# Two transformer layers on one core: where the streamed activations lie relative to the weights, modulo 128 bytes

## The chip, the core and the metric

The kernel runs on one core of a Trainium2 chip. The metric is the device time of one launch in microseconds. The kernel before took 2894.02 us, the median of three runs (2893.97, 2894.02 and 2896.38 us). A profile of one further execution stands beside them; where lines of the kernel are named (L213), they are those of the kernel before.

## What is computed

The input x has 256 tokens of 2048 numbers. Two layers follow each other. The first puts 16 learned tokens ahead, mixes with an RWKV-7 recurrence beside a causal attention, and ends with a gated feed-forward part. The second mixes with a long convolution (Hyena) beside a latent attention, and ends with a feed-forward part whose gate passes through a 3-tap convolution. Cut to the products that matter here:

```python
proj = rms(h) @ w_in                                   # 2048 x 10704
merged = g_a * (y_a @ w_branch_a) + g_b * (y_b @ w_branch_b)
h = h + merged @ w_o                                   # 2048 x 2048
gate, up = split(rms(h) @ w_gate_up)                   # 2048 x 11264
h = h + (silu(gate) * up) @ w_down                     # 5632 x 2048
proj = rms(h) @ w_in_2                                 # second layer
h = h + rms(concat(rms(y_hyena), rms(y_attn)) @ w_out_2)
g, u = split(rms(h) @ w_up_2)                          # 2048 x 11264
h = h + rms((gelu(conv3(g)) * u) @ w_down_2)           # 5632 x 2048
```

All is float32. Nearly all of the time goes into these dense products.

## The kernel before

**Split products.** TensorE multiplies numbers of reduced precision (fp32r), so each float32 operand is split into a high part (a rounded copy) and a low part (the rest). A product is three matmuls into the same PSUM bank (`mm3`, L213 to L215): weights high times activations high, weights low times activations high, weights high times activations low. The weights are the stationary operand, a 128x128 tile that LDWEIGHTS loads; the activations stream past as the moving operand, 256 columns (one per token) in most stages, 272 or 258 in the first product.

**The weight stream.** A weight matrix is cut into pieces of 8 tiles of 128x128 (512 KB). `stream` walks over the pieces and `weights` brings each: SP issues its DMA into `wr`, ScalarE casts it into `wh` (L195), VectorE subtracts into `wl` (L196). Each of the three has a pool of three buffers (`wraw`, `whi`, `wlo`) that all stages share. One piece feeds 8 x 3 = 24 matmuls. `weights` runs at high priority, so a scheduler puts the casts and subtractions well ahead of the rest of a stage; the order on each engine is fixed when the program is built.

**The stages**, in order: the first product (w_in, with the RWKV and attention work among it), `phase_merge` (w_ab, then w_o in `run`), `phase_glu` (w_gu, 176 pieces), w_down in `run` (176 pieces), `phase_mix` (w_in2 with the work of Hyena and of the latent attention), `phase_out` (w_out2), `phase_conv_glu` (w_up2, 176 pieces; its first four blocks run as one group while `bring` makes the normed activations) and `phase_last` (w_down2, 176 pieces). In `phase_last` the roles are turned: the hidden activations `hh` are stationary, 128 tokens at a time, and the weights move, 512 columns at a time (L925 to L927, 1056 matmuls).

**Where the operands lie.** A tile has the same byte address in every partition, and an allocator places tiles of a pool one behind the other. The helper `act` makes an activation tile 32 numbers (128 bytes) longer than needed and starts `off` numbers into it. `wr`, `wh` and `wl` start at 32 modulo 128 bytes in all their buffers, and each tile and each block of 256 columns is a multiple of 128 bytes long, so one number describes a stage: the start of the moving operand less that of the stationary one, modulo 128. This is called the **offset** below. In the built program before the change it is:

| stage | moving operand | matmuls | offset |
|---|---|---|---|
| w_in | xh, xl (272, 258 or 256 columns) | 5520 | changes by 64 from one k to the next |
| w_ab | yah, yal, ybh, ybl | 768 | 0 |
| w_o | mh, ml | 768 | 48 |
| w_gu | x2h, x2l | 4224 | 32 |
| w_down | hh, hl | 2112 | 64 |
| w_in2 | x3h, x3l | 1488 | 16 |
| w_q2, w_k2, w_v2 | hyh, hyl, huh, hul (w_v2: weights) | 216 | 0 |
| w_out2 | yhh, yhl, yah2, yal2 | 768 | 64 |
| w_up2 | x4h, x4l | 4224 | 96 |
| w_down2 | weights, 512 columns | 1056 | 96 |

The names yah and yah2 read alike in a profile (yah): before 1000 us it is the tile of w_ab, after 2000 us that of w_out2.

Of the kernel before, what the change touches and what calls it, by code (L numbers as in the profile page):

```python
# [12 lines left out]
F32R = mybir.dt.float32r  # L13
# [5 lines left out]
P = 128  # L19
D = 2048  # L20
KT = D // P
S = 256
# [6 lines left out]
HT = HID // P  # L29
C0 = math.exp(-0.5)  # L30
BIG = 1e30
PIECE = 8
# [118 lines left out]
class Builder:  # L151
# [21 lines left out]
    def act(self, pool, tag, off):  # L173

        return self.tl(pool, [P, KT * S + 32], tag, F32R)[:, off : off + KT * S].rearrange("p (k s) -> p k s", k=KT)

# [40 lines left out]
    def stream(self, name):  # L217

        w = self.a[name]
        for i in range(w.shape[0]):  # L220
            wh, wl = self.weights(w[i], PIECE)
            for k in range(PIECE):
                yield wh[:, k], wl[:, k]
# [78 lines left out]
    def run(self):  # L302
# [13 lines left out]
        al = slice(0, S)  # L316
        spill = nc.dram_tensor("spill_h", (P, KT, S), F32, kind="Internal").ap()
        spill2 = nc.dram_tensor("spill_h2", (P, KT, S), F32, kind="Internal").ap()
        with ExitStack() as right:
# [4 lines left out]
            with ExitStack() as pa:  # L324
                ph = ExitStack()
                php = self.pool(ph, "ph", side="right")
                self.h = self.tl(php, [P, KT, S], "h")
                pm = ExitStack()
                pmp = self.pool(pm, "pm", side="right")
                mh = self.act(pmp, "mh", 28)  # L330
                ml = self.act(pmp, "ml", 28)
                pf = ExitStack()
                filters = self.filters(pf)
                self.phase_merge(pa, mh, ml, filters)
            with ExitStack() as pb:
                xp = self.pool(pb, "x2")
                xh = self.act(xp, "x2h", 8)
                xl = self.act(xp, "x2l", 8)
# [15 lines left out]
            with ExitStack() as pc:  # L354
                xp = self.pool(pc, "x3")
                xh = self.act(xp, "x3h", 4)
                xl = self.act(xp, "x3l", 4)
                st = self.stream("w_down")
                for i in range(KT):
                    ps = self.bank()  # L360
                    self.dense(ps, st, HT, hh, hl, al)
                    self.residual(i, ps, "pre", xh, xl)
                    if i % 4 == 3:
                        nc.scalar.dma_start(out=spill[:, i - 3 : i + 1], in_=self.h[:, i - 3 : i + 1])
# [9 lines left out]
            with ExitStack() as pe:  # L374
                xp = self.pool(pe, "x4")
                xh = self.act(xp, "x4h", 24)
                xl = self.act(xp, "x4l", 24)
                php = self.pool(pe, "ph2")
                self.h = self.tl(php, [P, KT, S], "h")
                nc.scalar.dma_start(out=self.h, in_=spill)  # L380
                with ExitStack() as pf:
                    bring = self.phase_out(pf, ys, rs, xh, xl)
                    py.close()
                    pd = ExitStack()
                    hp = self.pool(pd, "hp2", side="right")
                    hh = self.tl(hp, [P, HT, S], "hh2", F32R)
                    hl = self.tl(hp, [P, HT, S], "hl2", F32R)
                    self.tl(hp, [P, 8], "shift")
                    self.phase_conv_glu(xh, xl, hh, hl, bring, spill2)
                self.dump("h3", self.h)  # L390
# [111 lines left out]
    def phase_merge(self, pa, mh, ml, filters):  # L502
        nc, a = self.nc, self.a
        al = slice(0, S)
        w = self.pool(pa, "pmgy")
        w2 = self.pool(pa, "pmg", 2)
        ys = []
# [31 lines left out]
    def phase_glu(self, xh, xl, hh, hl):  # L539
# [3 lines left out]
        with ExitStack() as c:  # L543
            w2 = self.pool(c, "pglu", 2)
            st = self.stream("w_gu")
# [319 lines left out]
    def phase_conv_glu(self, xh, xl, hh, hl, bring, spill):  # L865
# [3 lines left out]
        with ExitStack() as c:  # L869
            w2 = self.pool(c, "pcg", 2)  # L870
            st = self.stream("w_up2")
# [3 lines left out]
            for i in range(0, KT, 4):  # L875
                nc.scalar.dma_start(out=spill[:, i : i + 4], in_=self.h[:, i : i + 4])

# [521 lines left out]
```

## Time and profile before

| | |
|---|---|
| runs | 2893.97, 2894.02, 2896.38 us |
| profiled execution | 2894.61 us |
| its span, first to last instruction | 2892.8 us |
| mean granted TensorE clock | 0.995 |
| weight pieces: cast on ScalarE, subtraction on VectorE | 1045 ns and 1223 ns (mean of 872) |
| DMA of a piece of w_gu, issue to landing | 3.5 us (median) |

The profile's page gives busy time by engine, the chain of work that ended last and the costliest groups of instructions. For this change the most telling view is another: the busy time and the number of matmuls in a stretch of time. Where TensorE is busy all through, the length of the stretch over the number of matmuls that start in it is their spacing. The duration of one matmul in the other views is longer, since matmuls are pipelined and overlap.

### The profile page before, as it was taken

Reading aid. Unit: us, or ns where it says so; the run is one execution under the profiler, and the core shown is the slowest. Engines: PE = TensorE matmul, PEld = TensorE weight load, DVE = VectorE, ACT = ScalarE, POOL = GpSimd, SP = SyncE. Lnnn points to the kernel's source line nnn. Section 1 sums busy time; section 2 is a strip of 40 time slices with the busy share of each in tenths; the row PEclk is TensorE's granted clock in tenths of the full one; section 3 lists DMA queues with packets and bytes.
Section 4 is the critical chain, followed back from the end, with each engine's and each line's share of the span. In section 5 each row is a group of like instructions: output and inputs, shape, how many; then the busy total and the mean of one; then the engine's idle time right before and its main releaser. Section 6 shows DMA issues by size and latency. Waiting matters only on the chain.

```text
span 2892.8 us, 56251 instructions
## 1 busy us (share of the span) xinstructions
PE 2855.3 (99%) x23286; PEld 2688.2 (93%) x23286; DVE 1854.1 (64%) x2948; ACT 1340.9 (46%) x1998; POOL 184.8 (6%) x339
## 2 busy tenths in 40 slices
PE   8999999999999999999999999999989999999998
PEld 7988888888999999999999999999989999998886
DVE  8856666776566655555555556687786666665444
ACT  6544555555444444444444445444454444444433
POOL 4000000000000200000000000010220000000000
PEclk9999999999999999999999999999999999999999
DMA  6433333334676555555555666444655555556554
GB/s 209 135 113 112 99 116 106 114 105 134 194 241 200 185 183 188 184 186 186 185 187 199 202 200 216 160 144 146 198 177 187 185 187 183 189 184 222 187 188 160
DMA packets 147617, 497.23 MB, mean 172 GB/s; under 512 B 16224, under 2 KB 30816, under 8 KB 146784
## 3 DMA queue, kind: packets, MB, share of 16 engines
q1 hardware_dynamic: 128448, 458.42, 48.7%
q10 hardware_dynamic: 18272, 33.12, 3.3%
q8 instruction: 182, 2.98, 0.4%
q0 software_dynamic: 640, 2.10, 0.3%
q14 instruction: 75, 0.61, 0.1%
HBM read 478.37 MB, written 15.20 MB: 171 GB/s over the span
## 4 chain that ended last, share of the span: by engine, by line
PE 95%; DVE 2%; DMA 1%; ACT 1%; issue 0%; SPq 0%; POOL 0%; ACTq 0%; DVEq 0%; POOLq 0%
PE psd L215 12%; PE psd L213 12%; PE psd L214 12%; PE psb L213 5%; PE psb L215 5%; PE psa L215 5%; PE psc L213 5%; PE psa L213 5%; PE psc L214 5%; PE psc L215 5%; PE psb L214 5%; PE psa L214 4%; PE psd L926 1%; PE psd L925 1%; PE psa L926 1%; PE psa L925 1%
## 5 line engine op out<-in xcount | busy, mean ns | idle before, releaser
L196 DVE TENSOR_TENSOR wl<-wr,wh 128x1024 fp32r<-128x1024 f32 (+1 forms) x872 | 1065.9, 1223 | 668.5 <-ACT wh L195 667.4
L195 ACT CAST wh<-wr 128x1024 fp32r<-128x1024 f32 (+1 forms) x872 | 910.5, 1045 | 1241.5 <-PE psd L215 353.4
L214 PE MATMUL psd<-xh,wl 128*128 128x256 f32 (+2 forms) x1280 | 371.5, 290 | 0.2 <-DVE wl L196 0.2
L215 PE MATMUL psd<-xl,wh 128*128 128x256 f32 (+2 forms) x1280 | 371.4, 290 | 0.0
L213 PE MATMUL psd<-xh,wh 128*128 128x256 f32 (+2 forms) x1280 | 369.9, 289 | 0.6 <-DVE p L1000 0.6
L213 PEld LDWEIGHTS psd<-xh,wh 128*128 128x128 f32 x1280 | 241.2, 188 | 8.6 <-issue 4.1
L215 PEld LDWEIGHTS psd<-xl,wh 128*128 128x128 f32 x1280 | 241.1, 188 | 7.8 <-issue 3.2
L214 PEld LDWEIGHTS psd<-xh,wl 128*128 128x128 f32 x1280 | 240.9, 188 | 5.7 <-DVE wl L196 0.4
L213 PE MATMUL psd<-x3h,wh 128*128 128x256 f32 x496 | 141.3, 285 | 0.0
L215 PE MATMUL psd<-x3l,wh 128*128 128x256 f32 x496 | 140.5, 283 | 0.0
L214 PE MATMUL psd<-x3h,wl 128*128 128x256 f32 x496 | 139.8, 282 | 0.0
L256 POOL TENSOR_TENSOR acc<-acc,ssq 128x256 f32<-128x256 f32 x56 | 72.2, 1290 | 859.9 <-ACT ssq L258 859.8
L213 PE MATMUL psa<-x4h,wh 128*128 128x256 f32 x352 | 99.8, 284 | 3.8 <-ACT x4h L246 3.8
L214 PE MATMUL psa<-x4h,wl 128*128 128x256 f32 x352 | 99.7, 283 | 2.7 <-DVE wl L196 2.7
L215 PE MATMUL psa<-x4l,wh 128*128 128x256 f32 x352 | 99.3, 282 | 1.4 <-DVE x4l L247 1.0
L213 PE MATMUL psb<-x4h,wh 128*128 128x256 f32 x352 | 99.4, 282 | 0.0
L213 PE MATMUL psc<-x4h,wh 128*128 128x256 f32 x352 | 99.4, 282 | 0.0
L213 PE MATMUL psd<-x4h,wh 128*128 128x256 f32 x352 | 99.4, 282 | 0.0
L215 PE MATMUL psa<-x2l,wh 128*128 128x256 f32 x352 | 99.2, 282 | 0.0
L213 PE MATMUL psa<-x2h,wh 128*128 128x256 f32 x352 | 99.2, 282 | 0.0
L214 PE MATMUL psd<-x4h,wl 128*128 128x256 f32 x352 | 99.1, 282 | 0.0
L214 PE MATMUL psb<-x4h,wl 128*128 128x256 f32 x352 | 99.1, 282 | 0.0
(664 smaller groups left out, 8476.2 us busy)
## 6 DMA issues: line engine op xcount, KB each, us to landing
wr<-w_in_dram SPq DMA_DIRECT2D x230, 512.0 KB, 3.4
wr<-w_gu_dram SPq DMA_DIRECT2D x176, 512.0 KB, 3.5
wr<-w_down_dram SPq DMA_DIRECT2D x176, 512.0 KB, 3.5
wr<-w_up_dram SPq DMA_DIRECT2D x176, 512.0 KB, 3.5
wr<-w_ab_dram SPq DMA_DIRECT2D x32, 512.0 KB, 4.3
wr<-w_o_dram SPq DMA_DIRECT2D x32, 512.0 KB, 3.4
wr<-w_out_dram SPq DMA_DIRECT2D x32, 512.0 KB, 4.3
spill_g<-gate ACTq DMA_DIRECT2D x32, 128.0 KB, 2.7
```

Of the source, the lines that this page charges most:

```text
L195: self.nc.scalar.copy(hi, src)
L196: self.nc.vector.tensor_tensor(out=lo, in0=src, in1=hi.bitcast(F32), op=ALU.subtract)
L213: nc.tensor.matmul(out, lhsT=wh, rhs=xh, start=start, stop=False)
L214: nc.tensor.matmul(out, lhsT=wl, rhs=xh, start=False, stop=False)
L215: nc.tensor.matmul(out, lhsT=wh, rhs=xl, start=False, stop=stop)
L256: nc.gpsimd.tensor_tensor(out=acc, in0=acc, in1=self.pending[id(acc)], op=ALU.add)
L925: nc.tensor.matmul(ps[b], lhsT=hh[:, k, bs], rhs=wh[:, q], start=k == 0, stop=False)
L926: nc.tensor.matmul(ps[b], lhsT=hh[:, k, bs], rhs=wl[:, q], start=False, stop=False)
```

## The change

`act` is gone, and with it the numbers 28, 8, 4 and 24. Each activation pool of a streamed stage gets either nothing or a small tile `shift` of 64 bytes first, so that the operands lie at an offset of 64. The pool of hh2 loses its 32-byte `shift`. In the built program the offset is 64 in every row of the table above but w_in, whose rows stay as they were.

Second, `stream` takes a list of pieces that go "away": their high and low parts get a buffer of their own, outside the three, which lies at 96 modulo 128 as the activations do, so that these pieces are multiplied at an **offset of 0**. They are pieces 2, 6, 40 and 100 of w_gu, piece 2 of w_down and pieces 10, 14, 48 and 100 of w_up2: 9 of 528, 216 matmuls. Their raw data still pass through `wraw`.

Third, in `phase_conv_glu` the pool of `phase_out` (`pmo`, with `mix`) is closed after the group and before the pools `pcgw` and `pcg` are opened, so the away buffer and the tiles of the convolution (`conv_p`, `cg`, `cu`) lie where `mix` was.

```diff
-    def act(self, pool, tag, off):
-
-        return self.tl(pool, [P, KT * S + 32], tag, F32R)[:, off : off + KT * S].rearrange("p (k s) -> p k s", k=KT)
-
...
-    def stream(self, name):
+    def shift(self, pool):
+
+        self.tl(pool, [P, 16], "shift")
+
+    def stream(self, name, away=(), pool=None):
+
 
         w = self.a[name]
         for i in range(w.shape[0]):
-            wh, wl = self.weights(w[i], PIECE)
+            if i in away:
+                wh, wl = self.weights(w[i], PIECE, (self.wraw, pool[0], pool[0]), tag="aw")
+            else:
+                wh, wl = self.weights(w[i], PIECE)
             for k in range(PIECE):
                 yield wh[:, k], wl[:, k]
...
-                mh = self.act(pmp, "mh", 28)
-                ml = self.act(pmp, "ml", 28)
+                mh = self.tl(pmp, [P, KT, S], "mh", F32R)
+                ml = self.tl(pmp, [P, KT, S], "ml", F32R)
...
-                xh = self.act(xp, "x2h", 8)
-                xl = self.act(xp, "x2l", 8)
+                self.shift(xp)
+                xh = self.tl(xp, [P, KT, S], "x2h", F32R)
+                xl = self.tl(xp, [P, KT, S], "x2l", F32R)
...
-                xh = self.act(xp, "x3h", 4)
-                xl = self.act(xp, "x3l", 4)
-                st = self.stream("w_down")
...
+                self.shift(xp)
+                xh = self.tl(xp, [P, KT, S], "x3h", F32R)
+                xl = self.tl(xp, [P, KT, S], "x3l", F32R)
+                with ExitStack() as c:
+                    st = self.stream("w_down", (2,), [self.pool(c, "pdn")])
...
-                xh = self.act(xp, "x4h", 24)
-                xl = self.act(xp, "x4l", 24)
+                self.shift(xp)
+                xh = self.tl(xp, [P, KT, S], "x4h", F32R)
+                xl = self.tl(xp, [P, KT, S], "x4l", F32R)
...
-                    self.tl(hp, [P, 8], "shift")
-                    self.phase_conv_glu(xh, xl, hh, hl, bring, spill2)
...
+                self.phase_conv_glu(xh, xl, hh, hl, bring, spill2, pf)
...
         w = self.pool(pa, "pmgy")
+        self.shift(w)
...
+            st = self.stream("w_gu", (2, 6, 40, 100), [self.pool(c, "pgl")])
             w2 = self.pool(c, "pglu", 2)
-            st = self.stream("w_gu")
...
-            w2 = self.pool(c, "pcg", 2)
-            st = self.stream("w_up2")
+            pool = []
+            st = self.stream("w_up2", (10, 14, 48, 100), pool)
             first = [self.bank() for _ in range(4)]
             self.group(first, st, KT, xh, xl, [al] * 4, bring)
             self.rstd(R, self.total(self.acc), S, 1.0 / D, 1e-6)
             for i in range(0, KT, 4):
                 nc.scalar.dma_start(out=spill[:, i : i + 4], in_=self.h[:, i : i + 4])
+            pf.close()
+            pool.append(self.pool(c, "pcgw"))
+            w2 = self.pool(c, "pcg", 2)
```

The order of instructions on TensorE is the same in both programs; only the names of the away tiles differ. On TensorE at piece 2 of w_gu, the end of piece 1 and the start of piece 2 now read (xh and xl of w_gu are x2h and x2l; the numbers are those of buffers):

```order
L211 MATMUL psa_12702<-x2l_11580,wh_12734 128x256
L209 MATMUL psa_12702<-x2h_11579,wh_12734 128x256
L210 MATMUL psa_12702<-x2h_11579,wl_12735 128x256
L211 MATMUL psa_12702<-x2l_11580,wh_12734 128x256
L209 MATMUL psb_12766<-x2h_11579,awh_12768 128x256
L210 MATMUL psb_12766<-x2h_11579,awl_12769 128x256
L211 MATMUL psb_12766<-x2l_11580,awh_12768 128x256
```

Nothing moved there: before, the same rows hold wh_12763 and wl_12764 in place of awh and awl.

On ScalarE at the end of w_o, the casts of w_gu's pieces 0, 1 and 2 (before: wh_12699, wh_12729 and wh_12763) stand among the last residuals:

```order
L195 CAST wh_12699<-wr_12698 128x1024
L258 ACTIVATE ssq_12604<-h_10059 128x256
L246 ACTIVATE x2h_11577<-h_10059,cols_61 128x256
L195 CAST wh_12729<-wr_12728 128x1024
L195 CAST wh_12763<-wr_12762 128x1024
L258 ACTIVATE ssq_12671<-h_10059 128x256
```

With the change they are wh_12704, wh_12734 and awh_12768:

```order
L191 CAST wh_12704<-wr_12703 128x1024
L262 ACTIVATE ssq_12606<-h_10059 128x256
L250 ACTIVATE x2h_11579<-h_10059,cols_61 128x256
L191 CAST awh_12768<-wr_12767 128x1024
L191 CAST wh_12734<-wr_12733 128x1024
L191 CAST wh_12798<-wr_12797 128x1024
```

The cast of the away piece, piece 2, now stands ahead of that of piece 1, which TensorE needs first; the subtractions on VectorE follow the same order.

On GpSimd, where `bring` adds up squares (acc, ssq) and `conv_p` gets its two zero columns, the memsets of the first two conv_p tiles stood ahead of the last additions:

```order
L256 TENSOR_TENSOR acc_86<-acc_86,ssq_25531 128x256
L563 MEMSET conv_p_25994 128x1
L564 MEMSET conv_p_25994 128x1
L563 MEMSET conv_p_26008 128x1
L564 MEMSET conv_p_26008 128x1
L256 TENSOR_TENSOR acc_86<-acc_86,ssq_25657 128x256
```

Now they stand behind all of them:

```order
L260 TENSOR_TENSOR acc_86<-acc_86,ssq_25929 128x256
L260 TENSOR_TENSOR acc_86<-acc_86,ssq_25948 128x256
L571 MEMSET conv_p_26009 128x1
L572 MEMSET conv_p_26009 128x1
L571 MEMSET conv_p_26023 128x1
L572 MEMSET conv_p_26023 128x1
```

Four memsets moved past fourteen additions, since their tiles now lie where `mix` was.

More of the change, by code (lines that the diff above doesn't have):

```diff
@@ L355, in run @@
                 xp = self.pool(pc, "x3")
-                xh = self.act(xp, "x3h", 4)
-                xl = self.act(xp, "x3l", 4)
-                st = self.stream("w_down")
[L359 to L364, printed above, removed]
+                self.shift(xp)
[3 more added lines that the diff above has]
+                    st = self.stream("w_down", (2,), [self.pool(c, "pdn")])
+                    for i in range(KT):
+                        ps = self.bank()
+                        self.dense(ps, st, HT, hh, hl, al)
+                        self.residual(i, ps, "pre", xh, xl)
+                        if i % 4 == 3:
+                            nc.scalar.dma_start(out=spill[:, i - 3 : i + 1], in_=self.h[:, i - 3 : i + 1])
                 pd.close()
@@ L380, in run @@
                 nc.scalar.dma_start(out=self.h, in_=spill)
[L381 to L387, printed above, removed]
-                    self.tl(hp, [P, 8], "shift")
-                    self.phase_conv_glu(xh, xl, hh, hl, bring, spill2)
+                pf = ExitStack()
+                bring = self.phase_out(pf, ys, rs, xh, xl)
+                py.close()
+                pd = ExitStack()
+                hp = self.pool(pd, "hp2", side="right")
+                hh = self.tl(hp, [P, HT, S], "hh2", F32R)
+                hl = self.tl(hp, [P, HT, S], "hl2", F32R)
+                self.phase_conv_glu(xh, xl, hh, hl, bring, spill2, pf)
                 self.dump("h3", self.h)
@@ L863, in phase_out, with phase_conv_glu @@
         return bring
-    def phase_conv_glu(self, xh, xl, hh, hl, bring, spill):
+    def phase_conv_glu(self, xh, xl, hh, hl, bring, spill, pf):
         nc, a = self.nc, self.a
```

## The prediction

> **What bounds the kernel now.** I read the page first: its line of busy times, the clock by slices, the chain of work that ended last.
>
> ```profile
> PE 2855.3 (99%) x23286; PEld 2688.2 (93%) x23286; DVE 1854.1 (64%) x2948; ACT 1340.9 (46%) x1998; POOL 184.8 (6%) x339
> PEclk9999999999999999999999999999999999999999
> PE 95%; DVE 2%; DMA 1%; ACT 1%; issue 0%; SPq 0%; POOL 0%; ACTq 0%; DVEq 0%; POOLq 0%
> ```
>
> TensorE is busy for 2855 of 2892.8 us at a clock that is nearly always granted in full, and it makes up 95% of the chain. But a busy TensorE need not run at its peak, so the question is how far apart matmuls start. The view of busy time by stretches answers it. Its columns are the stretch, its length, busy us and (x instructions) of TensorE, of its weight load, VectorE, ScalarE and GpSimd, then clock and DMA.
>
> ```profile
> 802.00:830.00 28.00, 28.00 (x236) 28.00 (x235) 17.96 (x25) 11.47 (x15) 0.00 (x0) 1.00 0.82 260
> 956.00:1016.00 60.00, 60.00 (x522) 60.00 (x521) 40.08 (x44) 30.86 (x44) 15.41 (x11) 1.00 0.61 197
> 1020.00:1516.00 496.00, 496.00 (x4186) 495.95 (x4185) 284.59 (x352) 213.31 (x265) 0.00 (x0) 1.00 0.58 185
> 1521.00:1757.00 236.00, 236.00 (x2085) 236.00 (x2084) 124.74 (x118) 102.36 (x117) 19.54 (x14) 1.00 0.61 200
> 1771.50:1781.50 10.00, 10.00 (x87) 10.00 (x86) 7.88 (x10) 6.14 (x10) 3.05 (x2) 1.00 0.87 290
> 2156.00:2630.00 474.00, 474.00 (x4002) 474.00 (x4001) 325.71 (x473) 203.61 (x255) 5.56 (x84) 1.00 0.57 185
> 2660.00:2880.00 220.00, 220.00 (x944) 176.98 (x944) 98.28 (x83) 86.19 (x91) 0.00 (x0) 1.00 0.54 179
> ```
>
> The count also holds the two or so matmuls that were still running when a stretch began (one lasts about 280 ns at a spacing near 118), so I take 2.4 off, and 1.7 for 512 columns. Spacings by stage: w_ab, offset 0: 28/233.6 = 119.9 ns. w_o, 48: 60/519.6 = 115.5. w_gu, 32: 496/4183.6 = 118.6. w_down, 64: 236/2082.6 = **113.3**. w_in2, 16: 10/84.6 = 118.2. w_up2, 96: 474/3999.6 = 118.5. w_down2, 96 at 512 columns: 220/942.3 = 233.5. In w_gu, w_down and w_up2 the clock is 1.00, TensorE never idle, the matmuls 256 wide and the weights from the same buffers. What differs in the table of offsets is only where the moving operand lies. The one at 64 is the fastest. The durations of single matmuls say the same:
>
> ```profile
> L213 PE MATMUL psc<-x4h,wh 128*128 128x256 f32 x352 | 99.4, 282 | 0.0
> L213 PE MATMUL psd<-x2h,wh 128*128 128x256 f32 x352 | 99.0, 281 | 0.0
> L213 PE MATMUL psc<-hh,wh 128*128 128x256 f32 x176 | 48.6, 276 | 0.0
> ```
>
> So TensorE's spacing is the bound, and offset 64 can be had for 113.3 ns. But not always. Two stretches of w_out2, whose offset is 64 as well, grouped by line and shape (count | busy us, mean ns of one):
>
> ```profile
> L214 PE MATMUL psb<-yah,wl 128*128 128x256 f32 x7 | 2.0, 281 | 0.0
> L215 PE MATMUL psb<-yal,wh 128*128 128x256 f32 x7 | 2.0, 281 | 0.0
> ...
> L214 PE MATMUL psc<-yhh,wl 128*128 128x256 f32 x13 | 3.6, 276 | 0.0
> L215 PE MATMUL psb<-yal,wh 128*128 128x256 f32 x8 | 2.2, 276 | 0.0
> ```
>
> The first two rows are from 2024.2 to 2026.7 us, the others from 2036 to 2046 us. The same tile yal takes 281 ns in the one and 276 in the other. The timeline of the first stretch gives its spacing:
>
> ```profile
> 2024.36 0.28 PE L215 MATMUL psb<-yal,wh 128*128 128x256 f32 x1
> ...
> 2026.83 0.28 PE L215 MATMUL psb<-yal,wh 128*128 128x256 f32 x1
> ```
>
> Between these starts lie 21 matmuls: 2.47/21 = **117.6 ns**, held for the whole group. So offset 64 has two modes, a fast one (113.3) and a slow one (117.6), and the slow one is worth hardly more than offsets 32 or 96 (118.5). Whatever came before a run picks the mode. This decides the case.
>
> **The change part by part**, in the fast mode:
>
> *w_gu*: 176 pieces x 24 = 4224 matmuls. 4128 go from 118.6 to 113.3: 5.3 x 4128 = 21.9 us. The 96 of the four level pieces go from 118.6 to 119.9 (the row of w_ab): +0.1. Gain 21.8. In the slow mode it would be 1.0 x 4128 - 0.1 = 4.0.
>
> *w_up2*: the first 192 matmuls are the group that waits for `bring`:
>
> ```profile
> 2121.00:2154.00 33.00, 28.71 (x201) 27.08 (x202) 31.74 (x52) 19.64 (x41) 13.20 (x14) 0.90 0.46 160
> ```
>
> There VectorE is busy for 31.74 of 33 us and TensorE waits for it, so nothing is gained. Of the other 4032, 3936 gain 118.5 - 113.3 = 5.2: 20.5, less 0.1 for the level pieces: 20.4.
>
> *w_down2*, 512 columns: no run at offset 64 is in the trace. At offset 0 there is one, w_v2, whose timeline shows
>
> ```profile
> 1827.27 0.39 PE L649 MATMUL psa<-wl,huh 128*128 128x512 f32 x1
> ...
> 1829.99 0.39 PE L649 MATMUL psa<-wl,huh 128*128 128x512 f32 x1
> ```
>
> 12 matmuls in 2.72 us: 226.7 ns. The 256 further columns thus cost 226.7 - 119.9 = 106.8 over the 256-wide matmul at the same offset; added to 113.3 that estimates 220.1 at offset 64. Gain: (233.5 - 220.1) x 1056 = 14.2 us. Bounds: nothing, if it stays at 233.5; and twice 106.8 = 213.6, columns alone, 21.0. I take 220.1 because it uses the row of the same width. The Trainium skill, page "TensorE: Matmul & The Clock Gate", section "Back-to-back issue gap", puts a warm matmul at columns/2.4 + 2.5 ns, that is 215.8 for 512; by that the gain would be 18.7. No run here shows that spacing at 512 columns.
>
> *w_ab*: 768 matmuls, 119.9. The first half runs unbroken, 384 x 6.6 = 2.5; the second half is broken by the filters' own matmuls, which stay as they are, so I count the slow mode there: 384 x 2.3 = 0.9. Sum 3.4; bounds 1.8 and 5.1.
> *w_o*: only the last 540 run unbroken: 2.2 x 540 = 1.2; bounds -1.1 (slow) and 1.7.
> *w_in2, w_q2, w_k2*: 1680 matmuls at 118 to 120 between attention and Hyena work. Half of them at 113.3: 840 x 4.9 = 4.1, of which I keep 3.3 since TensorE also waits for others there; bounds 0 and 8.2.
> *w_down* is at 64 already; its level piece costs 24 x 6.6 = 0.2. *w_out2*: nothing. Both lose if their mode turns slow: 4.3 x 2088 = 9.0 and 4.3 x 768 = 3.3.
>
> *Order.* The away piece's cast stands ahead of piece 1's on ScalarE. Piece 1 comes 1.05 us (cast) later, and its subtraction 1.22 us; TensorE works 24 x 113 = 2.7 us on piece 0 meanwhile. I count 1 us for one stall (bounds 0 and 2.3). The memsets of conv_p moved behind `bring`'s additions: the last addition ends at 2148.75 and VectorE first writes conv_p at 2156.51, so four memsets of one column each have 7.8 us, under the chain of the normalisation: nothing.
>
> ```profile
> 2147.62 1.13 POOL L256 TENSOR_TENSOR acc<-acc,ssq 128x256 f32<-128x256 f32 x1 [1.62 <-ACT ssq L258]
> 2156.51 0.42 DVE L565 TENSOR_TENSOR conv_p<-psa,R 128x256 f32<-128x256 f32 x1
> L195 ACT CAST wh<-wr 128x1024 fp32r<-128x1024 f32 (+1 forms) x872 | 910.5, 1045 | 1241.5 <-PE psd L215 353.4
> L196 DVE TENSOR_TENSOR wl<-wr,wh 128x1024 fp32r<-128x1024 f32 (+1 forms) x872 | 1065.9, 1223 | 668.5 <-ACT wh L195 667.4
> ```
>
> *Supply.* At 113.3 a piece lasts 2.72 us, which w_down is fed at already, without idle time on TensorE. VectorE does more beside it in w_up2: 325.71 of 474 us, which becomes 72% of 453. w_down2 would use a piece in 12 x 220 = 2.64 us. That is enough.
>
> Sum: 21.8 + 20.4 + 14.2 + 3.4 + 1.2 + 3.3 - 0.2 - 1.0 = **63.1 us**. The profiled execution took 2894.61 us (span 2892.8 and 1.8 around it), 0.6 above the median of 2894.02. 2894.6 - 63.1 = 2831.5; I say **2832**.
>
> **The rivals.**
>
> *One long stage stays slow.* Then w_gu gives 4.0 instead of 21.8 (or w_up2 3.6 instead of 20.4), and the time is near 2850. For it: of the few runs at 64 in the trace two modes are seen, and none that leaves a level run without a wait. Against it: a level run, once settled, is perfectly regular, so what follows it should come out the same each time; and where w_in2 (16) follows a level tile directly, its first matmuls are at fast spacings:
>
> ```profile
> 1889.70 0.28 PE L215 MATMUL psc<-il,hyh 128*128 128x256 f32 x1
> 1889.82 0.28 PE L213 MATMUL psd<-x3h,wh 128*128 128x256 f32 x1
> 1889.94 0.28 PE L214 MATMUL psd<-x3h,wl 128*128 128x256 f32 x1
> 1890.05 0.28 PE L215 MATMUL psd<-x3l,wh 128*128 128x256 f32 x1
> 1890.16 0.28 PE L213 MATMUL psd<-x3h,wh 128*128 128x256 f32 x1
> ```
>
> 0.12, 0.12, 0.11, 0.11. So I take the level pieces for a way out of the slow mode; w_down entered the fast one from w_gu's uneven offset 32 without help.
>
> *The level pieces do nothing*, both long stages are slow, w_down stays fast: 4.0 + 3.6 + 3.4 + some 3 of w_down2 = 14, near 2880.
>
> *Slower than before.* The slow mode, once entered, is carried along: w_gu hands it to w_down, and w_out2 gets it too. Losses 9.0 + 3.3 + 1.1 + 0.2 + 1.0 = 14.6; gains 4.0 + 3.6 + 1.8 = 9.4, w_down2 nothing: +5.2, near 2900. It decides from the point where the long stages run above some 117 ns, since they must then pay for w_down's 113.3.
>
> *The offset doesn't matter* and the stages differ for another reason: 2894. The Trainium skill, page "TensorE: Matmul & The Clock Gate", section "Part 2: What happens when you issue a matmul", says so: two independent read ports, and loading the next weights takes nothing from the running matmul. The trace does not agree: 276 ns at 64 beside 281 and 282 at 32 and 96, everything else alike.
>
> **How the numbers follow.** Forecast, fast in all long stages: 0.62, from the bounds above 2817 (21.8 + 20.4 + 21.0 + 5.1 + 1.7 + 8.2 - 0.2 = 78.0) to 2852 (w_down2, w_in2 and w_o at nothing). One long stage slow: 0.17. Level pieces useless: 0.11. Offset without effect: 0.04. Slower: 0.06. The range 2817 to 2868 holds the first two cases but for their tails. A measurement of this kernel tells some 0.2% (6 us) from no change; by that faster 0.89, same 0.05, slower 0.06.
>
> **What would show it.** Right: matmuls of x2h, x4h and x3h at 276 ns, the 4224 matmuls of w_gu in some 479 us, the 4032 of w_up2 behind its group in some 457, w_down2 at 220 ns; the level pieces at 283 ns. A row of x2h or x4h that stays at 281 means the slow mode, and hh above 276 that it is carried on. TensorE waiting for wl would mean that supply took over. The estimate of 220.1 for 512 columns is the term most likely to be off.

## The result and the profile after

The changed kernel takes 2868.55 us (median of 4 runs, 2867.63 to 2870.97); the kernel before took 2895.05 beside it (4 runs). The ratio is 0.991, 95% interval 0.9892 to 0.9927. That is faster by 26.5 us, where 62 were forecast; the time lies half a microsecond above the range. The profiled execution has a span of 2865.8 us against 2892.8.

On the page, TensorE's busy time falls with the span, VectorE's and ScalarE's stay. The chain of waits has the same shares as before (TensorE 95%), so it is still TensorE's spacing that must be read.

```profile
PE 2827.8 (99%) x23286; PEld 2664.8 (93%) x23286; DVE 1852.2 (65%) x2948; ACT 1340.8 (47%) x1998; POOL 184.8 (6%) x339
```

The view by stretches, of the changed kernel, with the columns as above. The rows are w_o; three stretches of w_gu; w_down; three of w_up2; w_down2.

```profile
956.00:1016.00 60.00, 60.00 (x512) 60.00 (x511) 39.70 (x43) 30.36 (x45) 15.28 (x11) 1.00 0.59 197
1040.00:1110.00 70.00, 70.00 (x620) 70.00 (x619) 41.77 (x53) 31.37 (x39) 0.00 (x0) 1.00 0.56 184
1140.00:1280.00 140.00, 140.00 (x1191) 140.00 (x1190) 80.96 (x100) 59.35 (x75) 0.00 (x0) 1.00 0.57 188
1305.00:1500.00 195.00, 195.00 (x1723) 195.00 (x1722) 116.46 (x145) 86.64 (x108) 0.00 (x0) 1.00 0.59 193
1506.00:1750.00 244.00, 244.00 (x2074) 244.00 (x2073) 124.01 (x118) 100.53 (x116) 19.54 (x14) 1.00 0.59 194
...
2166.00:2240.00 74.00, 74.00 (x655) 74.00 (x655) 52.07 (x77) 32.86 (x41) 0.93 (x14) 1.00 0.56 188
2266.00:2385.00 119.00, 119.00 (x1013) 119.00 (x1012) 81.09 (x116) 50.58 (x63) 1.32 (x20) 1.00 0.56 187
2411.00:2605.00 194.00, 194.00 (x1714) 194.00 (x1714) 137.22 (x196) 86.66 (x108) 2.25 (x34) 1.00 0.59 194
2640.00:2850.00 210.00, 210.00 (x919) 172.30 (x918) 97.02 (x82) 85.14 (x90) 0.00 (x0) 1.00 0.56 186
```

With 2.4 (1.7 for 512 columns) off the count as before: w_o 60/509.6 = 117.7 ns (was 115.5). w_gu 113.3, then **117.8**, then 113.3 again. w_down **117.8** (was 113.3). w_up2 113.4, 117.8, 113.3. w_down2 210/917.3 = 228.9 (was 233.5; forecast 220). The clock is 1.00 in every row and TensorE never idle. So there are the two modes of offset 64 that the prediction spoke of, and no third thing; they are only not where it put them. Single matmuls grouped by line and shape show the same (w_gu in its first fast stretch, then w_down):

```profile
L209 PE MATMUL psa<-x2h,wh 128*128 128x256 f32 x61 | 16.8, 276 | 0.0
...
L209 PE MATMUL psb<-hh,wh 128*128 128x256 f32 x176 | 49.5, 281 | 0.0
```

From the starts in the timeline each piece (24 matmuls) can be called fast (113.3 ns) or slow (117.8). (w_down's 2112 matmuls make 88 pieces, numbered 0 to 87, and w_down2 has 88 as well; the 176 given for these two above is wrong.) Fast are pieces 3 to 5, 7 to 38 and 101 to 175 of w_gu, 11 to 13, 15 to 46 and 101 to 175 of w_up2, and none of w_down. The level pieces themselves, those at offset 0, take 120 ns a matmul in w_gu and w_up2 and 118.6 in w_down, and are left out.

Where does the fast mode end in w_gu? Not at level piece 40, but in piece 39. The timeline there (start in us, duration, engine, line, tiles):

```profile
1124.62 0.28 PE L211 MATMUL psd<-x2l,wh 128*128 128x256 f32 x1
1124.74 0.28 PE L209 MATMUL psd<-x2h,wh 128*128 128x256 f32 x1
1124.85 0.28 PE L209 MATMUL psa<-x2h,awh 128*128 128x256 f32 x1
1124.97 0.28 PE L210 MATMUL psd<-x2h,wl 128*128 128x256 f32 x1
1125.09 0.28 PE L211 MATMUL psd<-x2l,wh 128*128 128x256 f32 x1
1125.21 0.28 PE L209 MATMUL psd<-x2h,wh 128*128 128x256 f32 x1
```

The third row reads awh: it is the first matmul of level piece 40, and it stands *inside* piece 39, ahead of matmuls of another bank. Up to it starts lie 0.11 to 0.12 apart, behind it 0.12; piece 39 as a whole takes 117.8 ns a matmul and piece 38 takes 113.3. **The section on the change is wrong here**: it says that the order on TensorE is the same in both programs. I had looked at piece 2, where that holds. At pieces 40 and 100 of w_gu and 48 and 100 of w_up2, each the first of a block with a new bank, the scheduler put one matmul ahead (not at 2, 6, 10 and 14, though these begin a block as well), as its order shows for piece 39 (names with buffer numbers):

```
L209 MATMUL psd_13936<-x2h_11579,wh_13968 128x256
L209 MATMUL psa_14002<-x2h_11579,awh_14004 128x256
L210 MATMUL psd_13936<-x2h_11579,wl_13969 128x256
L211 MATMUL psd_13936<-x2l_11580,wh_13968 128x256
```

Where w_down begins, the starts widen at the very first matmuls of hh:

```profile
1503.86 0.28 PE L210 MATMUL psd<-x2h,wl 128*128 128x256 f32 x1
1503.98 0.28 PE L211 MATMUL psd<-x2l,wh 128*128 128x256 f32 x1
1504.09 0.28 PE L209 MATMUL psa<-hh,wh 128*128 128x256 f32 x1
1504.21 0.28 PE L210 MATMUL psa<-hh,wl 128*128 128x256 f32 x1
1504.33 0.28 PE L211 MATMUL psa<-hl,wh 128*128 128x256 f32 x1
```

0.12, 0.11, 0.12, 0.12: no wait, and the slow mode from there on; its level piece 2 changes nothing.

### The profile page after: what moved, and what is told of

The parts are those of the page before. It is cut to its first block, busy times and chain, and to the rows that moved or that the text cites. A ratio compares the mean times of both kernels' runs of the same rounds, so it can differ in the third digit from the quotient of the medians.

```text
span 2865.8 us, 56247 instructions
## 1 busy us (share of the span) xinstructions
PE 2827.8 (99%) x23286; PEld 2664.8 (93%) x23286; DVE 1852.2 (65%) x2948; ACT 1340.8 (47%) x1998; POOL 184.8 (6%) x339
## 4 chain that ended last, share of the span: by engine, by line
PE 95%; DVE 2%; DMA 1%; ACT 1%; issue 0%; SPq 0%; POOL 0%; ACTq 0%; DVEq 0%; POOLq 0%
PE psd L211 12%; PE psd L210 12%; PE psd L209 12%; PE psb L209 5%; PE psb L211 5%; PE psb L210 5%; PE psa L211 5%; PE psc L210 5%; PE psa L210 5%; PE psa L209 4%; PE psc L209 4%; PE psc L211 4%; PE psa L937 1%; PE psd L938 1%; PE psd L937 1%; PE psa L938 1%
## 5 line engine op out<-in xcount | busy, mean ns | idle before, releaser
L192 DVE TENSOR_TENSOR wl<-wr,wh 128x1024 fp32r<-128x1024 f32 (+1 forms) x863 | 1055.1, 1223 | 642.8 <-ACT wh L191 641.5
L191 ACT CAST wh<-wr 128x1024 fp32r<-128x1024 f32 (+1 forms) x863 | 900.9, 1045 | 1199.0 <-PE psd L211 345.4
L209 PEld LDWEIGHTS psd<-x3h,wh 128*128 128x128 f32 x496 | 93.2, 188 | 2.7 <-ACT huh L191 1.3
L210 PE MATMUL psc<-x4h,wl 128*128 128x256 f32 x344 | 95.5, 278 | 0.0
L210 PE MATMUL psa<-x2h,wl 128*128 128x256 f32 x344 | 95.5, 278 | 0.0
```

The lines of the kernel that those rows point to most:

```text
L191: self.nc.scalar.copy(hi, src)
L192: self.nc.vector.tensor_tensor(out=lo, in0=src, in1=hi.bitcast(F32), op=ALU.subtract)
L209: nc.tensor.matmul(out, lhsT=wh, rhs=xh, start=start, stop=False)
L210: nc.tensor.matmul(out, lhsT=wl, rhs=xh, start=False, stop=False)
```

## The experiments

Eleven runs of ten kernels. Those executed once have no interval; the kernel before took 2894.8 to 2899.5 us beside them, on four chips, so what follows rests on the spacing within a stage rather than on totals. What is said of single pieces is read from one profiled execution of each run. "Fast 7 to 175" means pieces at 113.3 ns. All diffs are against the changed kernel.

### Fewer level pieces (few)

```
-            st = self.stream("w_gu", (2, 6, 40, 100), [self.pool(c, "pgl")])
+            st = self.stream("w_gu", (2, 6), [self.pool(c, "pgl")])
-            st = self.stream("w_up2", (10, 14, 48, 100), pool)
+            st = self.stream("w_up2", (10, 14), pool)
-                    st = self.stream("w_down", (2,), [self.pool(c, "pdn")])
+                    st = self.stream("w_down", (), [self.pool(c, "pdn")])
+                self.tl(hp, [P, 16], "pad")
```

> Level pieces only where the changed kernel's stay whole: w_gu 2 and 6, w_up2 10 and 14, none in w_down; hh2 moved by 64 bytes, so that w_down2 lies level (offset 0). Theory A (one matmul of a later level piece, which the program's order puts into the piece before it, turns the fast mode into the slow one): w_gu stays at 113.3 ns from piece 7 to its end, w_up2 from piece 15; against the changed kernel 60 and 52 pieces gain 24 x 4.45 ns each, 6.4 and 5.6 us, and four level pieces 0.6. Theory B (the fast mode lapses by itself after some 30 pieces): w_gu and w_up2 are slow from piece 39 and 47 to the end, which adds 75 pieces x 24 x 4.45 = 8 us to each. w_down, entered from a fast piece at the same offset as in the changed kernel: 117.8 by both. w_down2 at offset 0: 226.7 as w_v2 showed, 2.3 us less than at 64. In all 2854 by A, 2882 by B.

2862.12 us. The stretches of w_gu, w_down, w_up2 and w_down2:

```profile
1040.00:1490.00 450.00, 450.00 (x3973) 450.00 (x3972) 269.64 (x332) 200.18 (x249) 0.00 (x0) 1.00 0.60 193
1500.00:1740.00 240.00, 240.00 (x2040) 240.00 (x2039) 122.57 (x115) 99.83 (x115) 19.52 (x14) 1.00 0.59 194
2160.00:2590.00 430.00, 430.00 (x3796) 430.00 (x3795) 304.54 (x436) 190.27 (x238) 5.16 (x78) 1.00 0.59 193
2640.00:2840.00 200.00, 200.00 (x863) 162.15 (x862) 91.98 (x78) 80.43 (x86) 0.00 (x0) 1.00 0.56 187
```

450/3970.6 = 113.3 and 430/3793.6 = 113.4: w_gu is fast 7 to 175 and w_up2 15 to 175. The fast mode doesn't lapse; the late level pieces had ended it, as theory A has it. w_down stays at 117.8. The total is 8 us above A's number: w_down2 at offset 0 takes 200/861.3 = 232.2, not 226.7 (3.5 us more than at 64, where I expected 2.3 less), and w_out2 was slow from its piece 7 on in this execution (25 x 24 x 4.45 ns = 2.7).

w_out2 has no level piece in any run. What stands in its piece 7 is a wait of TensorE for VectorE. The timeline of few at that place, and the stretches behind it in the changed kernel and in few:

```profile
2031.62 0.28 PE L209 MATMUL psd<-yah,wh 128*128 128x256 f32 x1
2032.54 0.39 PE L210 MATMUL psd<-yah,wl 128*128 128x256 f32 x1 [0.65 <-DVE wl L192]
...
2042.00:2104.00 62.00, 62.00 (x550) 62.00 (x549) 42.90 (x59) 28.12 (x35) 15.78 (x12) 1.00 0.63 203
...
2036.00:2098.00 62.00, 62.00 (x528) 62.00 (x528) 40.98 (x56) 26.87 (x34) 15.04 (x11) 1.00 0.60 194
```

Ahead of the wait both are fast (113.3). Behind it the changed kernel, whose starts lie 0.75 us apart there, is fast (62/547.6 = 113.2); few, with 0.92 us, is slow (62/525.6 = 118.0), and so are late_moved (0.59) and old_entry (0.80). The other runs that came fast to this wait left it fast, with 0.67 to 1.26 us. The step from yhh to yah, which comes one matmul ahead of the wait, is made at piece 5 as well and turned nothing there. So at such a wait the fast mode can end too, and the length of the wait alone does not decide.

### Late level pieces inside a block (inside)

```
+            st = self.stream("w_gu", (2, 6, 41, 101), [self.pool(c, "pgl")])
+            st = self.stream("w_up2", (10, 14, 49, 101), pool)
+                    st = self.stream("w_down", (3, 14, 25, 36, 47, 58, 69, 80), [self.pool(c, "pdn")])
+                self.tl(hp, [P, 24], "pad")
```

> The later level pieces one place on (41 and 101, 49 and 101), in the middle of a block of 16 tiles, where none of their matmuls is put ahead; in w_down level pieces 3, 14, 25 and so on to 80, all inside blocks; hh2 moved by 96 bytes (w_down2 at offset 32). Theory A (only the matmul put ahead turns the mode): w_gu and w_up2 stay at 113.3 ns beyond the four pieces but for these themselves (120), as in the run without them. Theory B' (a level piece met in the fast mode far into a stage ends it): slow from 42 to 100 and from 50 to 100, 486 and 495 us as in the changed kernel. w_down starts slow (117.8); a level piece turned slow to fast 4 times of 4 where it was whole in w_gu and w_up2, but not in w_down at piece 2: if that was chance of the phase, one of the eight turns it, gain 3 to 9 us; if level pieces don't work in w_down, 249 us as now. w_down2 at offset 32: 233 (as 96), 4.7 us more. In all near 2856 by A, 2870 by B'.

2856.61 us. w_gu behind level piece 41; w_down ahead of its level piece 14 and behind it; w_down2 at offset 32:

```profile
1142.00:1290.00 148.00, 148.00 (x1308) 148.00 (x1307) 88.87 (x109) 66.71 (x83) 0.00 (x0) 1.00 0.58 193
...
1500.00:1535.00 35.00, 35.00 (x299) 35.00 (x298) 19.10 (x19) 15.30 (x19) 1.64 (x1) 1.00 0.58 192
1546.00:1565.00 19.00, 19.00 (x170) 19.00 (x170) 11.55 (x13) 9.76 (x12) 2.98 (x2) 1.00 0.64 208
2640.00:2840.00 200.00, 200.00 (x855) 160.77 (x854) 90.22 (x77) 78.70 (x84) 0.00 (x0) 1.00 0.55 180
```

148/1305.6 = 113.4: a level piece that is whole, met in the fast mode, leaves it fast, at 41, 101 (w_gu), 49, 101 (w_up2) and six times in w_down. The later place wasn't the trouble, the matmul put ahead was. In w_down level piece 3 left it slow (35/296.6 = 118.0), 14 turned it (19/167.6 = 113.4), and it stayed so. So a level piece can turn w_down; at piece 2 it had not. Nor does one and the same level piece always act: w_up2's piece 10 left it slow in few, inside and late_moved and turned it in the changed kernel and in old_entry. w_down2 at 32 takes 234.4.

### No level pieces (none), and own places that are not level (own_buffer)

In the first the lists are empty. In the second the lists are the changed kernel's, and the own place is pushed on by 64 bytes:

```
+    def away(self, ctx, name):
+        p = self.pool(ctx, name)
+        self.shift(p)
+        return p
...
-            st = self.stream("w_gu", (2, 6, 40, 100), [self.pool(c, "pgl")])
+            st = self.stream("w_gu", (2, 6, 40, 100), [self.away(c, "pgl")])
...
```

(and the same in w_down and w_up2).

> No level piece in any stage; all offsets as in the changed kernel. If the level pieces are what brings the fast mode: w_gu and w_up2 slow throughout (117.8 ns), each 110 pieces x 24 x 4.45 = 11.7 us longer than in the changed kernel, in all 2891. If the streams become fast without them: 113.3, 2850. w_down is entered from a slow piece here: if it starts fast, the stage before decides how it starts; if slow, the entry at offset 64 itself does.

> The same pieces (w_gu 2, 6, 40, 100; w_down 2; w_up2 10, 14, 48, 100) go to a place of their own, but 64 bytes on, so that they are at offset 64 like all others; TensorE's order, with the matmuls put ahead, is that of the changed kernel. If being level is what acts: no piece turns the mode, as without level pieces, 2891. If the own buffer or the order of casts and subtractions acts: the modes of the changed kernel, fast 7 to 38 and 101 to 175, 2868.

Without them: 2894.05 us, nothing gained. w_gu, w_down and w_up2 are slow from end to end (460/3905.6, 240/2037.6 and 470/3990.6, each 117.8):

```profile
1040.00:1500.00 460.00, 460.00 (x3908) 460.00 (x3907) 265.10 (x328) 196.99 (x245) 0.00 (x0) 1.00 0.57 187
1520.00:1760.00 240.00, 240.00 (x2040) 240.00 (x2040) 122.25 (x116) 100.27 (x115) 19.58 (x14) 1.00 0.59 193
2160.00:2630.00 470.00, 470.00 (x3993) 470.00 (x3992) 324.91 (x471) 203.88 (x256) 5.60 (x84) 1.00 0.57 187
```

With own places at offset 64: **2849.18 us**, better than the change, and neither of the two numbers that I had put down. I had held that being level is what turns the mode, or else that the modes would come out as in the change. The stretch of w_gu that was slow, and w_down:

```profile
1140.00:1280.00 140.00, 140.00 (x1238) 140.00 (x1237) 83.53 (x105) 62.93 (x78) 0.00 (x0) 1.00 0.58 193
...
1510.00:1736.00 226.00, 226.00 (x1996) 226.00 (x1996) 120.06 (x113) 98.41 (x113) 19.55 (x14) 1.00 0.61 199
```

140/1235.6 = 113.3 and 226/1993.6 = 113.4. w_gu is fast 2 to 175, w_down 3 to 87, w_up2 14 to 175. The one matmul still stands ahead in piece 39, now at offset 64:

```profile
1126.31 0.28 PE L209 MATMUL psd<-x2h,wh 128*128 128x256 f32 x1
1126.43 0.28 PE L209 MATMUL psa<-x2h,awh 128*128 128x256 f32 x1
1126.54 0.28 PE L210 MATMUL psd<-x2h,wl 128*128 128x256 f32 x1
1126.65 0.28 PE L211 MATMUL psd<-x2l,wh 128*128 128x256 f32 x1
```

0.12, 0.11, 0.11: it does no harm. Same order, same tile, only 64 bytes on. So the order alone isn't what ends the fast mode; the single matmul must also be level. And to leave the slow mode, no level piece is needed: in w_gu the spacing falls at the first matmul of own piece 2, in w_down at the first one behind own piece 2. I call this theory C: a change of the place that weights come from can turn slow into fast, and, at offset 64, has not turned fast into slow. It is not shown to the end: the own places also change the order of casts and subtractions, which was not varied alone. What speaks for the place is that the spacing changes with the first matmul that reads from it or the first one behind it (in own_few's w_up2 three matmuls later).

### More own places (own_all)

```
+        st = self.stream("w_ab", (2, 10, 18, 26), [self.away(pa, "pab")])
+                own = [self.away(pb, "po")]
+                st = self.stream("w_o", (2, 10, 18, 26), own)
...
+                    st = self.stream("w_down", (2, 6), [self.away(c, "pdn")])
+            st = self.stream("w_up2", (10, 14), pool)
...
```

and in w_down2 the high halves of pieces 3 and 14 of each quarter in an own place.

> As own_buffer, with more pieces at a place of their own at offset 64: w_ab and w_o 2, 10, 18, 26, w_down 2 and 6, w_up2 10 and 14, and in w_down2 the high halves of pieces 3 and 14 of each quarter. Theory C (a change of the place that weights come from, at offset 64, turns slow into fast in some of its occurrences and never fast into slow): w_gu and w_down fast from piece 2 or 3 as in own_buffer; w_o, slow (117.8) from piece 7 on in own_buffer, turns at one of the places 10 to 27, gain 24 x 4.45 ns for each piece after it, 1 to 2.2 us; w_ab the same order, 1 us. w_down2 holds 228.9 ns in own_buffer: if that is its slow mode, it turns to 220 to 227 in some quarter, 2 to 9 us less; if it has only one, nothing. In all 2838 to 2847. Theory D (own_buffer's modes were chance, not the places): w_o and w_ab stay slow and w_gu or w_down may be slow again, 2849 to 2870.

2843.07 us. Two parts came out otherwise: w_gu turned at own piece 6, where piece 2, at the same address as in own_buffer, had left it slow (w_gu shares w_o's own place here), and the own places of w_ab turned nothing. w_o turns fast at piece 11, behind own piece 10 (60/527.6 = 113.7); w_down2 is not moved by its eight own places (180/786.3 = 228.9):

```profile
950.00:1010.00 60.00, 60.00 (x530) 60.00 (x529) 38.90 (x43) 29.85 (x43) 14.07 (x11) 1.00 0.59 193
2640.00:2820.00 180.00, 180.00 (x788) 147.71 (x787) 82.96 (x71) 73.92 (x80) 0.00 (x0) 1.00 0.58 190
```

So 228.9 is the only spacing that w_down2 has shown at offset 64, and offset 64 is the best of the four tried there (0: 232.2, 32: 234.4, 96: 233.5).

### Place or distance (own_few, own_apart)

own_few keeps own pieces 3 and 175 of w_gu and 14 of w_up2. own_apart lets the low half lie 12288 bytes behind the high half, as in the stream's three buffers, where it was 4096 in own_buffer:

```
+    def apart(self, ctx, name):
+        p = self.pool(ctx, name)
+        self.tl(p, [P, 2 * PIECE * P], "gap")
+        return p
...
-                wh, wl = self.weights(w[i], PIECE, (self.wraw, pool[0], pool[0]), tag="aw")
+                wh, wl = self.weights(w[i], PIECE, (self.wraw, pool[0], pool[-1]), tag="aw")
```

> Only piece 3 and the last one, 175, of w_gu and piece 14 of w_up2 at a place of their own (offset 64), none in w_down. Theory C: w_gu turns fast at piece 3 or 4, and stays (one occurrence of two turned it in own_buffer's w_down). w_up2: fast from 14 or 15. w_down: the pieces at its start were slow in all five kernels at offset 64, whether w_gu ended fast or slow; so if the change of the moving operand sets it, it is slow throughout even behind the place of piece 175 (249 us, 9.5 more than own_buffer); if the weights' place just ahead matters, it is fast (239.5). In all 2859 or 2849. Theory D: other modes in w_gu and w_up2, up to 2891.

> As own_buffer in w_gu and w_down, but the low half of an own piece lies 12288 bytes behind its high half, as in the stream's own buffers, and not 4096; in w_up2 only piece 11. If the place of the weights is what turns the mode: w_gu fast from piece 2, w_down from 2 or 3, 2850. If the distance between the high and low half does: w_gu and w_down slow throughout, 18 and 9 us more, 2877.

own_few: 2857.31 us. One own piece is enough in w_gu (fast from 3) and in w_up2 (within 14). w_down, behind own piece 175 and with none of its own, is slow throughout: 240/2037.6 = 117.8.

```profile
1500.00:1740.00 240.00, 240.00 (x2040) 240.00 (x2039) 122.54 (x115) 99.85 (x115) 19.52 (x14) 1.00 0.59 192
```

own_apart: 2865.13 us. w_gu and w_down are fast from the same pieces as in own_buffer, 2 and 3, so the distance between the halves is not what turns them. w_up2 with its only own piece at 11 is slow to the end (430/3650.6 = 117.8), which is the difference of 16 us to own_buffer:

```profile
1040.00:1490.00 450.00, 450.00 (x3973) 450.00 (x3973) 269.31 (x332) 199.68 (x249) 0.00 (x0) 1.00 0.59 193
...
2160.00:2590.00 430.00, 430.00 (x3653) 430.00 (x3653) 293.43 (x419) 183.75 (x229) 5.04 (x76) 1.00 0.57 187
```

### The late level pieces elsewhere (late_moved)

```
+            st = self.stream("w_gu", (2, 6, 60), [self.pool(c, "pgl")])
+            st = self.stream("w_up2", (10, 14, 70), pool)
+                    st = self.stream("w_down", (14,), [self.pool(c, "pdn")])
```

> Level pieces of the changed kernel again (offset 0), but the late ones of w_gu and w_up2 elsewhere: 60 and 70, both at the start of a block, so that the program puts their first matmul into the piece before (second matmul of 59 and of 69); in w_down piece 14 alone. Theory A (a single level matmul among matmuls at 64 turns fast into slow): w_gu fast up to that matmul in 59, w_up2 up to 69, slow behind it; whether level piece 60 or 70 then turns it back is open (100 did, 40 and 48 didn't). If not: 116 and 106 pieces at 24 x 4.45 more than in the run named few. Rival (40 and 48 are special places, or some 30 fast pieces are the limit): fast to the end, or slow from near 39 and 47. w_down: turned fast by piece 14 as in the run named inside, 7.8 us less than in few; w_down2 back at 64, 3.7 less. Near 2875 by A without a turn back, 2851 if nothing turns it.

2874.22 us, where A gave 2875. w_gu is fast 7 to 58 and slow from the matmul put ahead in 59, w_up2 fast 15 to 68 and slow from 69. The stretches of w_gu ahead of it and behind it, and the timeline at the place:

```profile
1040.00:1180.00 140.00, 140.00 (x1238) 140.00 (x1237) 84.13 (x104) 62.67 (x78) 0.00 (x0) 1.00 0.57 190
1190.00:1500.00 310.00, 310.00 (x2635) 310.00 (x2634) 178.59 (x219) 131.49 (x165) 0.00 (x0) 1.00 0.57 186
```

```profile
1179.93 0.28 PE L209 MATMUL psb<-x2h,wh 128*128 128x256 f32 x1
1180.05 0.28 PE L209 MATMUL psc<-x2h,awh 128*128 128x256 f32 x1
1180.17 0.28 PE L210 MATMUL psb<-x2h,wl 128*128 128x256 f32 x1
1180.29 0.28 PE L211 MATMUL psb<-x2l,wh 128*128 128x256 f32 x1
```

140/1235.6 = 113.3, then 310/2632.6 = 117.8. The place of the turn follows the matmul put ahead, in both stages. One part came out otherwise: w_down, which I expected slow up to 14, is fast from its first piece here, behind a slow w_gu (14 pieces, 1.5 us).

### The old entry into w_down (old_entry)

```
-                self.shift(xp)
-                xh = self.tl(xp, [P, KT, S], "x2h", F32R)
-                xl = self.tl(xp, [P, KT, S], "x2l", F32R)
+                xh = self.act(xp, "x2h", 8)
+                xl = self.act(xp, "x2l", 8)
...
+            st = self.stream("w_gu", (), [self.pool(c, "pgl")])
+                    st = self.stream("w_down", (), [self.pool(c, "pdn")])
```

(mh and ml likewise at their old place, w_up2 with pieces 10 and 14.)

> x2h, x2l and mh, ml back at their places of before (offset 32 in w_gu, 48 in w_o), no level pieces in w_gu and w_down; w_up2 with pieces 10 and 14 level; the rest as in the changed kernel. If what w_down starts with is set by the stage ahead of it (an uneven w_gu at 32 hands over the fast mode, as before the change; a fast w_gu at 64 handed over the slow one in nine executions of nine): w_gu 118.5 throughout, 501 us, w_down fast from its first piece, 239.3; w_o 115.5, 1 us less than in the changed kernel. Against the run named few: +21.4 -9.3 -1.0 -3.7 (w_down2 at 64) = 2870. If w_down's start is chance, or its place beside the moved buffers makes it slow: 248.6, in all 2879.

2871.09 us. w_o, w_gu and w_down:

```profile
956.00:1016.00 60.00, 60.00 (x522) 60.00 (x521) 40.38 (x44) 30.60 (x44) 15.42 (x11) 1.00 0.61 196
1020.00:1510.00 490.00, 490.00 (x4135) 489.95 (x4134) 281.24 (x348) 210.84 (x262) 0.00 (x0) 1.00 0.56 185
1530.00:1750.00 220.00, 220.00 (x1943) 220.00 (x1943) 117.29 (x112) 96.09 (x111) 19.57 (x14) 1.00 0.61 201
```

115.5, 118.6 and 113.4. With w_gu back at 32, w_down is fast from its first piece. w_down itself is as in the run few, with its operands at the same addresses, and there it was slow. What differs is what stands ahead of it; that this sets the mode rests on this one execution and the kernel before.

### A version that beats both (own_places, own_again)

own_places is own_all without own places in w_down2, with more in w_ab and w_o; own_again is own_buffer once more.

```
+        st = self.stream("w_ab", (2, 6, 10, 14, 18, 22, 26, 30), [self.away(pa, "pab")])
+                st = self.stream("w_o", (2, 6, 10, 14, 18), own)
+            st = self.stream("w_gu", (2, 6, 10), own)
+                    st = self.stream("w_down", (2, 6), [self.away(c, "pdn")])
+            st = self.stream("w_up2", (10, 14), pool)
```

> The version that the runs point to: no level pieces; own places at offset 64 in w_ab (2, 6, 10, 14, 18, 22, 26, 30), w_o (2, 6, 10, 14, 18), w_gu (2, 6, 10), w_down (2, 6) and w_up2 (10, 14). Theory C: w_o turned fast by one of its five, w_gu by 10, w_down by 3, w_up2 by 14: as own_all, 2843, or up to 2 us less if w_ab's further places turn it earlier; ratio to the kernel before 0.981 to 0.983. Theory D (own_all's modes were chance): 2850 to 2870.

> The kernel of own_buffer once more, timed in rounds: if what turns the mode is fixed by the program, its time and the pieces at which the mode turns come again (2849, w_gu from 2, w_down from 3, w_up2 from 14); if chance, they differ from execution to execution by up to 18 us a stage.

own_places: 2845.98 us (5 runs, 2841.99 to 2850.79), own_again: 2847.21 (4 runs, 2846.32 to 2848.36), the kernel before 2894.78 (9 runs). Both have the ratio 0.9838 (0.9825 to 0.9851 and 0.9824 to 0.9851), against 0.991 for the change. The long stages turned at the same pieces as foreseen: 6, 3 and 14; 2, 3 and 14. In w_o own_places turned at 11 as own_all did, and in w_ab at 6. The median of own_places is 3 us above the 2843 expected and its ratio just above the 0.981 to 0.983; the execution profiled is the fastest of its five, and which pieces turned in the others isn't known. The extra own places in w_ab and w_o can't be told from none of them in the time; the five runs spread over 9 us.

## Why the prediction was right and wrong

The stages' lengths, from the first matmul of one to that of the next in the two timelines, in us:

| stage | before | after | gain | forecast |
|---|---|---|---|---|
| w_ab | 116.9 | 114.9 | 2.0 | 3.4 |
| w_o | 99.9 | 100.9 | -1.0 | 1.2 |
| w_gu | 501.2 | 486.6 | 14.6 | 21.8 |
| w_down | 239.6 | 249.0 | -9.4 | -0.2 |
| phase_mix | 257.9 | 256.2 | 1.8 | 3.3 |
| w_out2 | 104.5 | 104.3 | 0.2 | 0 |
| w_up2 | 510.2 | 495.5 | 14.7 | 20.4 |
| w_down2 | 249.7 | 245.0 | 4.7 | 14.2 |
| order | | | 0 | -1.0 |

With 0.6 us lost ahead of w_ab this makes the 27.0 of the two spans.

*The bound and the two modes: right.* TensorE's spacing alone moved the time. In w_gu, w_down and w_up2 of the changed kernel offset 64 gave 113.3 or 117.8 ns and nothing between over whole pieces, and the gain of these stages follows from counting pieces. For w_gu, against 118.6 before: 110 fast pieces x 24 x 5.3 ns, 62 slow ones x 24 x 0.8, four level ones x 24 x -1.4: 14.0 + 1.2 - 0.1 = 15.1, where 14.6 was measured.

*The step that failed: "I take the level pieces for a way out of the slow mode"*, with "what follows it should come out the same each time". I reasoned as if a level piece could only help. The runs show three things in its place. First, a single level matmul among matmuls at 64 turns fast into slow (after: 39, 47; late_moved: 59, 69), while a whole piece does not (inside) and a single one at 64 does not (own_buffer). That costs w_gu and w_up2 their pieces 39 to 99 and 47 to 99: 60 and 52 x 24 x 4.45 ns = 6.4 and 5.6 us, of misses of 7.2 and 5.7. I could have seen it in the order at pieces 40, 48 and 100, and looked only at piece 2. Second, a level piece doesn't turn the mode each time: 40, 48, 60 and 70 did not, nor w_down's 2, and w_up2's 10 did in two runs of five. Third, being level is not what does it; a place of its own at 64, where nothing is level, does as well or better. What in that place acts is not shown.

*w_down, costed at -0.2: the second miss, 9.2 us.* The prediction had the number ("4.3 x 2088 = 9.0", if its mode turns slow) and gave it to a rival of 0.06, because I read "w_down entered the fast one from w_gu's uneven offset 32 without help" as a property of w_down. The runs point to what stands ahead of it. Behind w_gu at 32 w_down starts fast (before, old_entry); behind a fast w_gu at 64 it started slow in all nine executions profiled here. Behind a slow w_gu at 64 it was slow once (none) and fast once (late_moved), so the mode of w_gu alone doesn't settle it. Why stays open. The price belonged into the sum's range together with w_gu's gain, since in these runs the one came with the other.

*w_down2, 14.2: a size.* Right sign, a third of the size. The step "220.1 at offset 64", w_v2's 106.8 for 256 more columns put on 113.3, failed: it is 228.9, and even the row that it started from doesn't carry over, since w_down2 at w_v2's offset 0 takes 232.2 and not 226.7. Twelve matmuls of another product were too few to lean on; why 512 columns cost 228.9 stays open. The Trainium skill, page "TensorE: Matmul & The Clock Gate", section "Back-to-back issue gap", has 215.8 by its formula, which it gives for a single matmul; for a stream of weight loads and matmuls it gives some 131 ns instead. Neither is met here: the smallest that a run shows at 512 columns in a long stream is 228.9.

*w_o, w_ab and w_out2.* w_o is the slow bound of its term: 2.2 ns x 540 lost at 117.7 beside 115.5 (old_entry has 115.5 back). w_ab and phase_mix came out at a little over half, slow for most of their pieces. That w_out2 lost nothing was in part luck: in four of the eleven runs it was slow behind its wait.

*Order.* No stall was added. The only uneven starts in piece 1 of w_gu, 362 and 306 ns apart, lie around two matmuls of another product (the sum of ssq, L271) between which TensorE does not wait; they were 361 and 305 before.

*The range.* Its end of 2852 for the first case is misadded: without w_down2, w_in2 and w_o the terms leave 44.4 us, which gives 2850.

*The rivals.* What happened is a mixture of two that I kept apart, a part of each long stage slow, and w_down slow; each had its price worked out, but no case held both. The mechanism given with the second, a slow w_gu that hands its mode to w_down, is not what happened: w_gu ended fast and w_down began slow.

## What to carry to other kernels

Where TensorE is busy without a gap, measure the spacing of its starts stage by stage before taking it for the peak; here one and the same stream ran at 113.3 or 117.8 ns, by where its operands lie and by what ran just ahead of it. A change that gains by such a state must be costed at every border where the state may be lost: the stage behind, a wait, and each instruction that a scheduler may lift out of its group, so the order has to be read at every place the change touches and not at one. And test the cheap variant of a remedy with its supposed cause taken out: the own place at 64 bytes on was worth twenty microseconds more than the level one.

## What was not expected of the hardware

A stream of matmuls with nothing else changed holds either mode for thousands of matmuls (w_gu 2 to 175 fast in own_buffer, 0 to 175 slow in none); two matmuls of another product among those of piece 1 of w_gu did not turn it in none, nor does the step from one to the next of the stream's three buffers, which every piece makes. One piece (24 matmuls) from another place does, at particular pieces: w_up2's own piece 14 turned it in each of the five runs that had one, its own piece 10 in none of four and 11 not in the one that had it; w_gu's own piece 2, at one address, turned it in three runs and left it slow in two. What distinguishes 14 from 10 stays open; so does whether the reads of the two operands collide at all, since no run here looks below the matmul. The Trainium skill, page "TensorE: Matmul & The Clock Gate", section "Part 2: What happens when you issue a matmul", has two independent read ports, so that loading the next weights takes nothing from the running matmul. By that the place of the weights should not matter, and the runs don't agree: w_gu takes 117.8 ns a matmul in none and 113.3 in own_buffer, whose w_gu differs only in where the weights of four pieces lie and in the order that follows from it.
